# Experts' biases: 128-row products for gate and up, one sum over all tokens for down, and four pairs of split weights beside nine raw slots

## The chip, the cores and the metric

The kernel runs on one core of one Trainium2 chip. The metric is the device time of one execution in microseconds (us). The engines are named as in the profile: PE (TensorE, its matmuls; PEld its weight loads), DVE (VectorE), ACT (ScalarE), POOL (GpSimd) and SP (SyncE, which issues most of the DMAs).

## The reference, cut to what matters

The program computes one block with four mixers and a routed feed-forward part, and then a second block of two layers. The change touches the feed-forward part of the first: 512 tokens of 1024 features, 32 experts, four experts for each token.

```python
logits = (x2d @ router_w + router_b).astype(jnp.float32)
top_val, top_idx = lax.top_k(logits, TOP_K)
gate = jax.nn.softmax(top_val, axis=-1)
...
hg, hl = jnp.split(xblk @ w_gu[e] + b_gu[e], 2, axis=-1)
hg = jnp.minimum(hg, SWIGLU_LIMIT)
hl = jnp.clip(hl, -SWIGLU_LIMIT, SWIGLU_LIMIT)
glu = hg * jax.nn.sigmoid(hg * SWIGLU_ALPHA)
return ((hl + 1.0) * glu) @ w_down[e] + b_down[e]
...
y = (yb * row_gate[:, None]).astype(x2d.dtype)
return jnp.zeros((t + 1, d), x2d.dtype).at[row_tok].add(y)[:t]
```

All of it is float32 and is kept at nearly that precision: a float32 operand is cut into a high and a low part of the type float32r, and a product is the sum of three (high times high, low times high, high times low).

## The kernel before

`block1_ffn` holds the part in question. It first makes the output projection, the layer norm and the router for the four token tiles, then runs over the 32 experts, then adds a gated embedding and a second norm by token tile.

An expert has 96 slots for tokens (`NS`). `slots` finds the tokens of an expert's slots: four one-hot tiles `o1` (L1378), four small bf16 products (L1380), and a few narrow vector operations that give the index `ix`, the destination `dx` and the gate `gc`. It also makes `sel`, a tile of 64 rows whose columns all have a one at rows e and 32 + e (L1375, on POOL, from `eye2`). `rows` gathers the tokens (`xg`, L1397) and transposes them into two parts `xT` (`transposed`, L1227 on PE, L1228 on ACT, L1229 on DVE).

`main` computes the expert. For each half q of the hidden features and for gate and up, it begins a bank `gu` with the product of `sel` and `bias` (L1411: 64 rows, high and low parts of all the experts' biases, one above the other), and adds 8 blocks of 128 features by `mm3` (L1148 to L1150, three products each of 512 columns). Then come, for each half, `hg` (L1421, DVE, from the gate bank), `sg` (L1422, ACT), `hg` times `sg` (L1424, POOL), `hl` (L1423, DVE, from the up bank), `hl` again (L1425, DVE), and the transposition of `hl` into `hT`. The down product `py` begins with two products of `sel` and `bdn` (L1432, 64 rows), and adds 2 times 8 blocks by `mm3`. `y` is `py` times the gate, and an indirect DMA adds it to the rows of `h_d` (L1444). The last expert goes another way: `last` keeps its rows in two parts, and `add_last` (L1501 on) adds them by one-hot products to the token tiles.

The weights come in units of 128 by 2048 float32 (1 MB), 12 for each expert: 8 for gate and up, 4 for down. SP issues the loads (L1201) in the order of use into slots that take turns: 6 in the ring, 1 and `N_SPARE` more, in all 11 (L1636). `unit` splits each: ACT copies it to `wh` (L1210), DVE subtracts to get `wl` (L1211). There are `N_PARTS` pairs of `wh` and `wl`, three. So a raw slot is free when `wl` is done, and a pair is free when PE has done the unit's 12 products.

The order of the instructions on each engine is fixed when the program is built, by a scheduler that has its own estimates of what each takes; at run time an engine runs its list in that order and waits where an operand isn't there. So PE passes from one expert to the next without a stop: between the products of one expert stand the biases, transposes and one-hot products of the next.

Of the kernel before, what the change touches and what calls it, by code (L numbers as in the profile page):

```python
# [8 lines left out]
F32 = mybir.dt.float32  # L9
F32R = mybir.dt.float32r  # L10
# [9 lines left out]
D = 1024  # L20
# [3 lines left out]
# ---------------------------------------------------------------- host layout  # L24
# Feature tiles (128 output columns of w_in each) and token-major groups (256).
# [7 lines left out]
FT = [  # name, columns (-1: zero)  # L33
# [93 lines left out]
def layout(inp):  # L127
    """The inputs laid out for the loads: transposed, cut and padded with zeros."""
# [59 lines left out]
    # experts, in units in the order of use: half, gate or linear, k half; k half, half  # L188
# [10 lines left out]
# ---- second block: 16 meta tokens and 512 tokens, 528 in all  # L199
# [18 lines left out]
def _ret_cols(base, j, f=None):  # L218
    """columns of a tile with heads 2j, 2j+1: halves of 24 at rows 0, 32 and 64, 96"""
# [25 lines left out]
def _ret_tables():  # L245
    """rotary tables with the decay gamma^(t - 264) (q) and gamma^(264 - t) / sqrt(dk) (k) folded in"""
# [19 lines left out]
def layout2(inp, o):  # L266
# [6 lines left out]
    o["w2o"] = ft(I("w_out"))          # [2, 8, 128, 8, 128]  # L273
    o["w21"] = ft(I("w_ffn1"))         # [2, 22, 128, 8, 128]
    o["w23"] = ft(I("w_ffn3"))
    w2 = I("w_ffn2").reshape(2, 22, 128, 8, 128)
    part = lambda a: np.ascontiguousarray(a.transpose(0, 3, 2, 1, 4))   # [2, 8, 128, tiles, 128]
# [46 lines left out]
# ---------------------------------------------------------------- device  # L324
# [30 lines left out]
def softplus_steps(k, pool, z, out):  # L355
    """out = softplus(z) = max(z, 0) + log1p(exp(-|z|))"""
# [17 lines left out]
def block1_mix(k, es_mix):  # L374
    """In-projection and the four mixers. Returns their outputs side by side, feature-major
    [128, 8, 512], in two float32r parts, in a pool of es_mix."""
    nc, tc, A = k.nc, k.tc, k.A
    V, ACT, G, PE = nc.vector, nc.scalar, nc.gpsimd, nc.tensor
    with ExitStack() as es:
# [28 lines left out]
        def wt(shape, name, bufs=1):  # L408
            """working tile; the larger ones share slots by size"""
# [44 lines left out]
        def tproj(name, evac):  # L454
            """one token tile at each step"""
# [24 lines left out]
        def tgate(name):  # L480
            """u * sigmoid(u)"""
# [21 lines left out]
        def conv(name, cw, cb, j, out):  # L503
            """out = silu(causal conv of width 4)"""
# [11 lines left out]
        # ---- row quantities: dt and the cumulated decay (SSD), gates (mLSTM)  # L516
# [38 lines left out]
        def post_norm(y, nh, eps, center, gname, mi, between=None, fast=False):  # L555
            """per-head norm over the features of y [128, NCH, 256] in place; then
            transposed into mix tiles mi, mi+1, with the gain (if gname)."""
# [34 lines left out]
        # ---- SSD  # L592
        def ssd():
# [6 lines left out]
            al = wt([128, NCH, 4], "al")     # exp(A_last), over all partitions  # L600
            dc = wt([128, NCH, 4], "dc")     # exp(A_last - A_s)
            ea = wt([128, NCH, 4], "ea")     # exp(A_t)
# [52 lines left out]
        # ---- GLA  # L655
        def gla():
# [15 lines left out]
            sc = wt([128, NCH], "gl_sc")     # state: end of chunk c to the middle of c+1  # L672
# [55 lines left out]
        # ---- mLSTM  # L728
        def mlstm():
# [11 lines left out]
            # the gate as tanh(u / 2) = 2 sigmoid(u) - 1  # L741
# [48 lines left out]
        # ---- the mixers' outputs and the weights of the output projection, two float32r parts each  # L790
# [8 lines left out]
        def out_piece(n, i):  # L799
            """two blocks of rows of half n of the columns"""  # L800
# [352 lines left out]
def block1_ffn(k, mix, wo, es_mix, b2):  # L1153
# [5 lines left out]
    with es:  # L1159
# [73 lines left out]
        with tile_pool(tc, name="w1", bufs=1) as w1:  # L1233
# [14 lines left out]
            for i in range(2):  # L1248
                nc.sync.dma_start(braw[32 * i:32 * i + 32], A["b_gu"])
# [1256 lines left out]
```

## Time and profile before

| | |
|---|---|
| time, median of 3 runs | 3178.87 us (3176.96 to 3190.85) |
| span of the profiled execution | 3183.1 us |
| PE busy | 3025.6 us, 95% of the span |
| DVE busy | 2144.0 us, 67% |
| ACT busy | 1533.5 us, 48% |
| POOL busy | 819.9 us, 26% |
| first `hg` of the first expert, of the last expert's second half | 488.7 us, 1717.0 us |

The share of busy time is taken over the whole span, whose stages differ. The experts take from about 450 to 1735 us. A matmul's own duration in a row is longer than the distance to the next one's start, since they overlap, so the cost of a product is read from the distance of the starts.

### The profile page before, as it was taken

The page shows a single profiled execution, that of the slowest core. Times are in us where ns is not written, and L with a number is a line of the kernel's source. Part 1 is how long each engine was busy: PE and PEld are TensorE (multiplying, and loading weights), DVE is VectorE, ACT ScalarE, POOL GpSimd, SP SyncE. Part 2 cuts the span into 40 slices and gives each one's busy share as a digit, 9 for nine tenths or more (in the row PEclk, how much of TensorE's full clock was granted, in tenths as well). Part 3 has the DMA queues.
Part 4 walks back from the last instruction along what each step waited for, and adds up shares of the span by engine and source line. Part 5 has one row for each costly group of instructions (what it writes and reads, how often), then busy time and mean ns, then how long its engine had stood idle before and what let it go on. Part 6 is the DMA issues. An engine that isn't in the chain of part 4 may idle for free. (4 is left out here: it accounts for less than half of the span.)

```text
span 3183.1 us, 45711 instructions
## 1 busy us (share of the span) xinstructions
PE 3025.6 (95%) x18347; PEld 2488.6 (78%) x18347; DVE 2144.0 (67%) x3036; ACT 1533.5 (48%) x1840; POOL 819.9 (26%) x538
## 2 busy tenths in 40 slices
PE   6899879999999999999999899999999899999997
PEld 4799666666666666666666788999999899999997
DVE  4745758999999989799988766653333846834324
ACT  4411426677766666676666644342222534432222
POOL 1210233333333333234322320320102501410104
PEclk8989889999999999999999989999999889999998
DMA  3201268999999999799997121122222211222221
GB/s 121 73 21 41 85 255 319 340 348 350 351 353 340 343 343 334 300 351 344 343 343 244 51 91 41 65 82 91 84 93 80 95 45 50 80 97 90 97 85 52
DMA packets 105991, 581.58 MB, mean 183 GB/s; under 512 B 13016, under 2 KB 13544, under 8 KB 55792
## 3 DMA queue, kind: packets, MB, share of 16 engines
q1 hardware_dynamic: 94784, 540.86, 45.9%
q0 software_dynamic: 10896, 37.52, 4.4%
q8 instruction: 145, 2.38, 0.3%
q14 instruction: 70, 0.57, 0.1%
q10 hardware_dynamic: 96, 0.26, 0.0%
HBM read 559.64 MB, written 18.94 MB: 182 GB/s over the span
## 5 line engine op out<-in xcount | busy, mean ns | idle before, releaser
L1211 DVE TENSOR_TENSOR wl<-w,wh 128x2048 fp32r<-128x2048 f32 (+1 forms) x398 | 909.3, 2293 | 85.0 <-ACT wh L1210 84.0
L1210 ACT ACTIVATE wh<-w 128x2048 fp32r<-128x2048 f32 (+1 forms) x410 | 734.1, 1808 | 133.2 <-PE gu L1150 87.1
L1775 PE MATMUL gu<-hh,w 128*128 128x256 f32 (+2 forms) x1552 | 454.6, 293 | 8.3 <-ACT hh L2473 8.3
L1776 PE MATMUL gu<-hl,w 128*128 128x256 f32 (+2 forms) x1552 | 451.3, 291 | 3.5 <-DVE hl L2475 2.7
L1777 PE MATMUL gu<-hh,w 128*128 128x256 f32 (+2 forms) x1552 | 449.1, 290 | 0.8 <-DVE w L1142 0.8
L1149 PE MATMUL gu<-wl,xT 128*96 128x512 f32 x1024 | 414.6, 405 | 8.8 <-DVE wl L1211 7.4
L1148 PE MATMUL gu<-wh,xT 128*96 128x512 f32 x1024 | 406.1, 397 | 0.2 <-ACT wh L1210 0.2
L1150 PE MATMUL gu<-wh,xT 128*96 128x512 f32 x1024 | 403.9, 394 | 0.0
L1142 DVE TENSOR_TENSOR w<-w 128x1024 fp32r<-128x1024 f32 (+1 forms) x190 | 237.6, 1251 | 234.1 <-ACT w L1141 229.8
L1141 ACT ACTIVATE w<-w 128x1024 fp32r<-128x1024 f32 (+1 forms) x194 | 201.2, 1038 | 259.5 <-PE gu L2299 84.6
L1775 PEld LDWEIGHTS gu<-hh,w 128*128 128x128 f32 x1552 | 300.6, 194 | 11.0 <-ACT hh L2473 9.9
L1776 PEld LDWEIGHTS gu<-hl,w 128*128 128x128 f32 x1552 | 300.0, 193 | 6.6 <-DVE hl L2475 4.4
L1777 PEld LDWEIGHTS gu<-hh,w 128*128 128x128 f32 x1552 | 300.9, 194 | 2.0 <-DVE w L1142 1.3
L1424 POOL TENSOR_TENSOR hg<-hg,sg 96x512 f32<-96x512 f32 x64 | 171.5, 2680 | 333.7 <-ACT sg L1422 333.7
L1149 PEld LDWEIGHTS gu<-wl,xT 128*96 128x96 f32 x1024 | 165.3, 161 | 106.6 <-DVE wl L1211 33.2
L2284 POOL TENSOR_TENSOR al<-fs,ah 128x528 fp32r<-128x528 f32 (+1 forms) x44 | 76.7, 1744 | 608.1 <-ACT ah L2283 608.1
L1148 PEld LDWEIGHTS gu<-wh,xT 128*96 128x96 f32 x1024 | 165.9, 162 | 73.4 <-issue 1.9
L1150 PEld LDWEIGHTS gu<-wh,xT 128*96 128x96 f32 x1024 | 165.8, 162 | 62.6
L1149 PE MATMUL py<-wl,hT 128*96 128x512 f32 x512 | 206.5, 403 | 0.2
L1148 PE MATMUL py<-wh,hT 128*96 128x512 f32 x512 | 204.3, 399 | 0.1
L1150 PE MATMUL py<-wh,hT 128*96 128x512 f32 x512 | 200.9, 397 | 0.0
L1444 POOL DMA_INDIRECT h_d<-y,dx x31 | 119.1, 3840 | 226.2 <-ACT y L1443 222.2
(701 smaller groups left out, 6478.0 us busy)
## 6 DMA issues: line engine op xcount, KB each, us to landing
w<-in_wgu SPq DMA_DIRECT2D x255, 1024.0 KB, 7.3
w<-in_wdn SPq DMA_DIRECT2D x127, 1024.0 KB, 6.5
w<-in_w SPq DMA_DIRECT2D x88, 512.0 KB, 3.5
w<-in_w2f SPq DMA_DIRECT2D x43, 512.0 KB, 3.7
w<-in_w22a SPq DMA_DIRECT2D x32, 512.0 KB, 3.8
w<-in_w1f SPq DMA_DIRECT2D x18, 512.0 KB, 3.5
w<-in_w2o SPq DMA_DIRECT2D x16, 512.0 KB, 3.6
w<-in_w22b SPq DMA_DIRECT2D x16, 384.0 KB, 3.4
```

What stands on the lines that cost most here:

```text
L1141: nc.scalar.activation(h, w, AF.Copy)
L1142: (eng or nc.vector).tensor_sub(l, w, h.bitcast(F32))
L1148: PE.matmul(out, a[0], b[0], start=start, stop=False)
L1149: PE.matmul(out, a[0], b[1], start=False, stop=False)
L1150: PE.matmul(out, a[1], b[0], start=False, stop=stop)
L1210: ACT.activation(h[:, j], w[:, j], AF.Copy)
L1211: (early or V).tensor_sub(l[:, j], w[:, j], h[:, j].bitcast(F32))
L1424: G.tensor_mul(hg, hg, sg)
L1444: G.indirect_dma_start(out=h_d, out_offset=bass.IndirectOffsetOnAxis(ap=dx[:, :1], axis=0), in_=y, in_offset=None, compute_op=OP.add)
L1775: PE.matmul(p, w[0][:, kk], x[0][:, kk, c], start=kk == ks[0], stop=False)
L1776: PE.matmul(p, w[0][:, kk], x[1][:, kk, c], start=False, stop=False)
L1777: PE.matmul(p, w[1][:, kk], x[0][:, kk, c], start=False, stop=kk == ks[-1])
```

## The change

- The biases of gate and up lie in `bias` as 128 rows of bf16: three parts one below the other (32 rows each, the rest of the rest), and 32 rows of zeros. `sel` has 128 rows of bf16 with three ones in each column. The product at the head of each `gu` bank thus has 128 rows instead of 64, and bf16 instead of float32r operands. Making the parts takes one copy on ACT, three subtractions and three casts of 32 by 2048 on DVE and a memset on POOL, where there was one copy and one subtraction. One DMA more brings the biases.
- The two products of `sel` and `bdn` are gone from each expert. The down biases are added once: `gates`, after the third expert's hidden features are there, transposes the gates of all tokens (four copies side by side) into `GT`, in parts; `add_last` begins each of its 8 banks with the product of `GT` and `bdn`, which now has 128 rows (high, high, low, low).
- `N_PARTS` goes from 3 to 4, `N_SPARE` from 4 to 2: four pairs of split weights, nine raw slots.
- `strict` has a tile and a DMA of its own. The loop over further blocks of experts, which is not run with these inputs, is changed to match.

Line numbers behind the diff differ from those above by 11 to 22. The comments, which the changed file drops, are left out.

```diff
-        bias = cons.tile([64, 2048], F32R, name="bias")
+        bias = cons.tile([128, 2048], BF, name="bias")
+        Gm = cons.tile([128, NCH, N_EXP], F32, name="Gm")
+        bdn = fcst.tile([128, D], F32R, name="bdn")
+        GT = fcst.tile([128, NCH, 128], F32R, name="GT")
...
-            braw = raw(rows=64)
-            for i in range(2):
+            braw = raw(rows=96)
+            for i in range(3):
                 nc.sync.dma_start(braw[32 * i:32 * i + 32], A["b_gu"])
-            ACT.activation(bias, braw, AF.Copy)
-            V.tensor_sub(bias[32:64], braw[32:64], bias[32:64].bitcast(F32))
+            ACT.activation(bias[0:96], braw, AF.Copy)
+            G.memset(bias[96:128], 0.0)
+            for i in range(1, 3):
+                b_, w_ = bias[32 * i:32 * i + 32], braw[32 * i:32 * i + 32]
+                for _ in range(i):
+                    V.tensor_sub(w_, w_, b_)
+                    V.tensor_copy(b_, w_)
...
-            for i in range(2):
+            for i in range(4):
                 nc.scalar.dma_start(bd[32 * i:32 * i + 32], A["b_dn"])
             ACT.activation(bdn, bd, AF.Copy)
-            V.tensor_sub(bdn[32:64], bd[32:64], bdn[32:64].bitcast(F32))
+            V.tensor_sub(bdn[64:128], bd[64:128], bdn[64:128].bitcast(F32))
+
+        def gates():
+            p = bank("tr", (128, 4, 128))
+            for t in range(NCH):
+                g4 = wb.tile([128, 128], F32, name="g4")
+                G.tensor_copy(g4.rearrange("p (a b) -> p a b", a=4), Gm[:, t][:, None, :].to_broadcast([128, 4, N_EXP]))
+                PE.transpose(p[:, t], g4, ident)
+            ACT.activation(GT, p, AF.Copy)
+            for i in (32, 96):
+                V.tensor_sub(GT[i:i + 32], p[i:i + 32], GT[i:i + 32].bitcast(F32))
...
-                sel = sm.tile([64, NS], F32R, name="sel", bufs=3)
-                eng.tensor_copy(sel, idc.to_broadcast([64, NS]))
+                sel = sm.tile([128, NS], BF, name="sel", bufs=3)
+                eng.tensor_copy(sel, idc.to_broadcast([128, NS]))
...
                 py = [bank("py", (NS, 512)) for _ in range(2)]
-                for n in range(2):
-                    PE.matmul(py[n], sel, bdn[:, 512 * n:512 * n + 512], start=True, stop=False)
...
-                            mm3(PE, py[n], (hT[0][:, a], hT[1][:, a]), (h[:, j], l[:, j]), False, a == 7)
+                            mm3(PE, py[n], (hT[0][:, a], hT[1][:, a]), (h[:, j], l[:, j]), a == 0, a == 7)
...
                     p = bank("py")
+                    PE.matmul(p, GT[:, t], bdn[:, 512 * n:512 * n + 512], start=True, stop=False)
                     for i in range(2):
-                        PE.matmul(p, oh[:, t], yp[:, D * i + 512 * n:D * i + 512 * n + 512], start=i == 0, stop=i == 1)
+                        PE.matmul(p, oh[:, t], yp[:, D * i + 512 * n:D * i + 512 * n + 512], start=False, stop=i == 1)
...
-                     {1: further, 20: embedding}.get(e), last if e == k.n_exp - 1 else None)
+                     {1: further, 2: gates, 20: embedding}.get(e), last if e == k.n_exp - 1 else None)
...
-N_RAW, N_SPARE, N_PARTS = 6, 4, 3
+N_RAW, N_SPARE, N_PARTS = 6, 2, 4
```

**On PE, in the middle of the experts.** Before, where the transposes of the next expert's tokens begin (`tr<-fcst,xg`), one of that expert's four gate and up biases (L1411) follows the transposes:

```order
L1148 MATMUL py<-wh,hT_7700 96x512
L1227 MATMUL tr<-fcst,xg 128x96 x4
L1411 MATMUL gu<-bias,sel 96x512
L1149 MATMUL py<-wl,hT_7700 96x512
L1150 MATMUL py<-wh,hT_7701 96x512
```

After, at the same place:

```order
L1148 MATMUL py<-wh,hT_7397 96x512
L1230 MATMUL tr<-fcst,xg 128x96 x4
L1433 LDWEIGHTS sel
L1433 MATMUL gu<-bias,sel 96x512
L1149 MATMUL py<-wl,hT_7397 96x512
```

The bias keeps its place among the products; as a bf16 product it has a weight load of its own in the list.

**On PE, a little later, where the down products of one expert end and the gate products of the next begin.** Before, one of the two down biases (L1432) stands behind the first gate product:

```order
L1149 MATMUL py<-wl,hT_7700 96x512
L1150 MATMUL py<-wh,hT_7701 96x512
L1148 MATMUL gu<-wh,xT_7658 96x512
L1432 MATMUL py<-bdn,sel 96x512
L1149 MATMUL gu<-wl,xT_7658 96x512
```

After:

```order
L1149 MATMUL py<-wl,hT_7397 96x512
L1150 MATMUL py<-wh,hT_7398 96x512
L1148 MATMUL gu<-wh,xT_7355 96x512
L1149 MATMUL gu<-wl,xT_7355 96x512
L1150 MATMUL gu<-wh,xT_7356 96x512
```

Nothing takes the place of the down bias.

**On DVE, in the start, around the second token tile's norm.** Before, one subtraction (L1251) for the biases stands between the two halves of that norm (L1103, L1104):

```order
L1103 SCALAR_TENSOR_TENSOR x<-x,rn_mv,g_3007 128x1024
L1251 TENSOR_TENSOR bias<-w,bias 32x2048
L1104 SCALAR_TENSOR_TENSOR x<-x,rn_rs,b_3008 128x1024
L1268 SCALAR_TENSOR_TENSOR x<-x,gu 128x512
L1096 BN_STATS rn_st<-x 128x6
L1288 TENSOR_TENSOR lg<-py,rb 128x32
```

After, six operations (L1261 and L1262) stand behind the norm, among the router's steps for that tile and the next tile's norm:

```order
L1104 SCALAR_TENSOR_TENSOR x<-x,rn_rs,b_3011 128x1024
L1279 SCALAR_TENSOR_TENSOR x<-x,gu 128x512
L1261 TENSOR_TENSOR w<-w,bias 32x2048 x2
L1262 CAST bias<-w 32x2048 x2
L1299 TENSOR_TENSOR lg<-py,rb 128x32
L1261 TENSOR_TENSOR w<-w,bias 32x2048
L1307 MAX m_3249<-lg 128x8
L1279 SCALAR_TENSOR_TENSOR x<-x,gu 128x512
L1262 CAST bias<-w 32x2048
```

The subtraction that stood ahead of the norm's second half is behind it, and five more operations stand ahead of the router's steps.

## Rows read from the trace of the kernel before

**Rows 1.** Windows, one expert each (first, second kind): busy us by engine, PE clock, DMA.
```profile
986.40:1025.63 39.23, 38.90 (x171) 25.04 (x170) 35.41 (x33) 26.27 (x20) 14.35 (x7) 1.00 0.96 342
720.25:758.21 37.96, 37.95 (x172) 25.31 (x171) 34.44 (x34) 26.83 (x21) 12.53 (x6) 1.00 0.96 353
```

**Rows 2.** One line's instructions each, L1411, L1432 and L1421: count, duration, first and last start.
```profile
L1411 PE MATMUL gu<-bias,sel x128: 383/466/473, 449.7 to 1688.0; 64*96 64x512 f32 x128
...
L1432 PE MATMUL py<-bdn,sel x64: 383/466/736, 474.6 to 1700.7; 64*96 64x512 f32 x64
...
L1421 DVE TENSOR_SCALAR hg<-gu x64: 673/680/689, 488.7 to 1717.0; 96x512 f32<-96x512 f32 x64
```

**Rows 3.** Timeline of PE, a gate or up bias alone: start, duration, instruction.
```profile
949.99 0.40 PE L1148 MATMUL gu<-wh,xT 128*96 128x512 f32 x1
950.31 0.47 PE L1411 MATMUL gu<-bias,sel 64*96 64x512 f32 x1
950.71 0.47 PE L1149 MATMUL gu<-wl,xT 128*96 128x512 f32 x1
951.02 0.39 PE L1150 MATMUL gu<-wh,xT 128*96 128x512 f32 x1
951.25 0.39 PE L1148 MATMUL gu<-wh,xT 128*96 128x512 f32 x1
```

**Rows 4.** Timeline of PE, two down biases side by side.
```profile
811.82 0.39 PE L1150 MATMUL gu<-wh,xT 128*96 128x512 f32 x1
812.14 0.70 PE L1432 MATMUL py<-bdn,sel 64*96 64x512 f32 x2
812.77 0.47 PE L1148 MATMUL py<-wh,hT 128*96 128x512 f32 x1
813.08 0.39 PE L1149 MATMUL py<-wl,hT 128*96 128x512 f32 x1
```

**Rows 5.** Timeline of PE, transposes and small bf16 products between the large ones.
```profile
826.13 0.49 PE L1227 MATMUL tr<-fcst,xg 96*128 96x96 f32 x4
826.46 0.30 PE L1380 MATMUL tr<-aux,o 128*96 128x6 bf16 x4
826.62 0.45 PE L1148 MATMUL gu<-wh,xT 128*96 128x512 f32 x1
```

**Rows 6.** The page's groups: the weight load of one of the large products.
```profile
L1149 PEld LDWEIGHTS gu<-wl,xT 128*96 128x96 f32 x1024 | 165.3, 161 | 106.6 <-DVE wl L1211 33.2
```

**Rows 7.** Timeline of PE, where a low part comes late.
```profile
992.32 0.40 PE L1148 MATMUL gu<-wh,xT 128*96 128x512 f32 x1
992.86 0.47 PE L1149 MATMUL gu<-wl,xT 128*96 128x512 f32 x1
```

**Rows 8.** Timeline of DVE beside it; in brackets the idle time before and its releaser.
```profile
986.40 0.69 DVE L1421 TENSOR_SCALAR hg<-gu 96x512 f32<-96x512 f32 x1 [1.05 <-PE gu L1150]
987.00 2.28 DVE L1211 TENSOR_TENSOR wl<-w,wh 128x2048 fp32r<-128x2048 f32 x1
989.65 3.15 DVE L1211 TENSOR_TENSOR wl<-w,wh 128x2048 fp32r<-128x2048 f32 x1 [0.37 <-ACT wh L1210]
```

**Rows 9.** Waits from 600 to 1600 us: who waited for whom, us in total, times, longest.
```profile
DVE wl L1211 <- ACT wh L1210: 70.9, 80, 10.6
ACT wh L1210 <- PE gu L1150: 66.0, 84, 1.6
```

**Rows 10.** SP's queue over the same stretch.
```profile
SPq L1201 <- DVE wl L1211: 820.8, 290, 7.0
```

**Rows 11.** Timeline of DVE in the start.
```profile
424.55 2.28 DVE L1251 TENSOR_TENSOR bias<-w,bias 32x2048 fp32r<-32x2048 f32 x1
...
443.98 0.19 DVE L1288 TENSOR_TENSOR lg<-py,rb 128x32 f32<-128x32 f32 x1 [3.94 <-PE py L1286]
```

**Rows 12.** Windows of 4 us inside the second kind of expert, columns as in rows 1.
```profile
736.00:740.00 4.00, 4.00 (x18) 2.50 (x17) 4.00 (x3) 1.98 (x2) 1.51 (x2) 1.00 1.02 422
...
752.00:756.00 4.00, 4.00 (x19) 2.80 (x18) 4.00 (x9) 3.23 (x2) 2.23 (x1) 1.00 0.58 158
```

More of the change, by code (lines that the diff above doesn't have):

```diff
@@ L1164, in block1_ffn @@
         fcst = pool("fcst", 1)
-        cst = fcst.tile([128, 256], F32, name="fcst")
+        ident = fcst.tile([128, 128], F32, name="fcst")
         pool_x = lambda n: es_x.enter_context(tile_pool(tc, name=n, bufs=1))
@@ L1171, in block1_ffn @@
         cst2 = cons.tile([128, 129], F32, name="fcst2")
-        ident, strict, iota, pidx = cst[:, 0:128], cst[:, 128:256], cst2[:, 0:128], cst2[:, 128:129]
-        bias = cons.tile([64, 2048], F32R, name="bias")
+        iota, pidx = cst2[:, 0:128], cst2[:, 128:129]
+        bias = cons.tile([128, 2048], BF, name="bias")
+        Gm = cons.tile([128, NCH, N_EXP], F32, name="Gm")
+        bdn = fcst.tile([128, D], F32R, name="bdn")
+        GT = fcst.tile([128, NCH, 128], F32R, name="GT")
         Rm = cons.tile([128, NCH, N_EXP], F32, name="Rm")
@@ L1207, in unit @@
             n = w.shape[1]
-            h, l = ((p or parts).tile([128, 4, 512], F32R, name=i, tag=i, bufs=1 if p else N_PARTS)[:, :n] for i in ("wh", "wl"))
+            h, l = (parts.tile([128, 4, 512], F32R, name=i, tag=i, bufs=N_PARTS)[:, :n] for i in ("wh", "wl"))
             for j in [slice(i, i + 1) for i in range(n)] if early else [slice(0, n)]:
@@ L1242, in block1_ffn @@
             nc.sync.dma_start(b1, bcast(A["rows2"], D, D))
-            nc.sync.dma_start(cst, A["cst"][:, 0:256])
+            strict = w1.tile([128, 128], F32, name="strict")
+            nc.sync.dma_start(ident, A["cst"][:, 0:128])
+            nc.sync.dma_start(strict, A["cst"][:, 128:256])
             nc.sync.dma_start(cst2, A["cst"][:, CF["iota"][0]:CF["iota"][0] + 129])
@@ L1255, in block1_ffn @@
             G.memset(ob_, 1.0)
-            eye2 = sm.tile([64, 32], F32, name="eye2")
-            V.tensor_add(eye2, ident[:64, 0:32], ident[:64, 32:64])
+            eye3 = sm.tile([128, 32], F32, name="eye3")
+            V.tensor_add(eye3, ident[:, 0:32], ident[:, 32:64])
+            V.tensor_add(eye3, eye3, ident[:, 64:96])
             M = w1.tile([128, NCH, N_EXP], F32, name="M")
             Mb = w1.tile([128, NCH, N_EXP], BF, name="Mb")
-            Gm = w1.tile([128, NCH, N_EXP], F32, name="Gm")
             for t in range(NCH):
@@ L1336, in block1_ffn @@
             wb = es_b.enter_context(tile_pool(tc, name="wb", bufs=1, side="right"))
-            bd = w1.tile([128, 8, 128], F32, name="x1T", bufs=2).rearrange("p a b -> p (a b)")[:64]
-            bdn = parts.tile([64, D], F32R, name="bdn")
-            for i in range(2):
+            bd = w1.tile([128, 8, 128], F32, name="x1T", bufs=2).rearrange("p a b -> p (a b)")
+            for i in range(4):
                 nc.scalar.dma_start(bd[32 * i:32 * i + 32], A["b_dn"])
             ACT.activation(bdn, bd, AF.Copy)
-            V.tensor_sub(bdn[32:64], bd[32:64], bdn[32:64].bitcast(F32))
+            V.tensor_sub(bdn[64:128], bd[64:128], bdn[64:128].bitcast(F32))
[8 more added lines that the diff above has]
+                V.tensor_sub(GT[i:i + 32], p[i:i + 32], GT[i:i + 32].bitcast(F32))
         def further():
@@ L1446, in main @@
                 return res
-            first = lambda e: slots(lambda t: Rm[:, t, e:e + 1], lambda t: aux[:, t, e], eye2[:, e:e + 1], G if e else V)
+            first = lambda e: slots(lambda t: Rm[:, t, e:e + 1], lambda t: aux[:, t, e], eye3[:, e:e + 1], G if e else V)
             def embedding():
@@ L1537, in block1_ffn @@
                     axe = ex.tile([128, NCH, 1, 6], BF, name="axe", bufs=1)
-                    ide = ex.tile([64, 1], F32, name="ide", bufs=1)
+                    ide = ex.tile([128, 1], F32, name="ide", bufs=1)
                     jc = ex.tile([128, 1], F32, name="jc", bufs=1)
@@ L1541, in block1_ffn @@
                     V.tensor_copy(axe, aux[:, :, bass.ds(e, 1)])
-                    V.tensor_copy(ide, eye2[:, bass.ds(e, 1)])
+                    V.tensor_copy(ide, eye3[:, bass.ds(e, 1)])
                     V.tensor_copy(jc, tblj[:, bass.ds(b, 1)])
```

## The prediction

> **What bounds the kernel now.** I read the windows first, one for each of two kinds of expert [rows 1]. Each runs from the first `hg` of one expert to that of the next, so its length is an expert's share of the time: 39.23 us for the one kind, 37.96 us for the other. In both PE is busy nearly throughout (38.90 and 37.95 us) at clock 1.00. DVE is not far behind: 35.41 and 34.44 us. ACT (26 us) and POOL (13 to 14 us) are not near. So PE sets the pace in this stage and DVE would be next, and the change takes work from PE there. Of the 31 distances from one expert to the next (64 `hg`, first and last in [rows 2]) 13 are of the first kind, 12 of the second, and 6 are others: the first two, and those around the embedding's projection.
>
> A busy PE is not PE at its peak, so I then read the starts of its products. Two plain products start 0.23 us apart (951.02 and 951.25 [rows 3]). A product of 64 rows between them takes more than its own place: the distance before it is 0.32, behind it 0.40, and the next one 0.31 us. From 949.99 to 951.02 that is 1.03 us for three products of which two are plain (0.46), so a bias that stands alone costs 0.57 us [rows 3]. Two side by side cost less: 1.26 us from 811.82 to 813.08, less two plain ones, is 0.80, or 0.40 each [rows 4].
>
> PE also waits a little. At 992.32 the distance to the next product is 0.54 instead of 0.23 us [rows 7]: that product needs `wl`, which DVE has in work just then, for 3.15 us instead of 2.28, and which it began late because `wh` was late [rows 8]. `wh` in turn waits for PE to give a pair free [rows 9]. This is a ring of three pairs with no room in it. An expert of the first kind has two such places, some 0.6 us together.
>
> **Gate and up biases.** 128 products of 64 rows [rows 2] become 128 of 128 rows. What a bf16 product of 128 rows and 512 columns costs among float32r ones, no row shows. From below it is a plain product, 0.23. From above it is what the 64-row one costs, 0.57, if the other type and not the fewer rows is what lengthens the distances. The nearest rows are the four small bf16 products of 128 rows that follow four transposes: 0.16 us for all four [rows 5]. They speak for the lower end, and I take 0.23. That saves 0.34 for a bias that stood alone and 0.17 for one of a pair: 4 x 0.34 = 1.4 us in an expert of the first kind, where all stand alone, and some 0.8 in one of the second.
>
> **Down biases.** 64 products go: 2 x 0.57 = 1.1 us in an expert of the first kind, 0.8 in one of the second. What takes their place lies outside the loop: eight products of 128 rows in `add_last`, 1.8 to 3.2 us by 0.23 and 0.40, some of it beside waits; I take +1.7. `gates` runs once: four transposes (0.33 by [rows 5], wider here) and two narrow DVE operations, at most 0.69 each as `hg` with the same 512 columns [rows 8]. That is 0 to 2; I take +0.5.
>
> **Fourth pair, two raw slots fewer.** A fourth pair lets ACT and DVE run one unit further ahead, which is 12 products or 2.8 us of PE. The late places (0.6 us) should go, and much of DVE's own waiting for `wh` (70.9 us over some 26 experts [rows 9]). The price is in the loads. SP's queue waits for a free slot nearly always, 820.8 us in 290 waits over 1000 us [rows 10], so loads run as far ahead as the slots permit. At 3 us for a unit, nine slots come round after 27 us where eleven took 33, and a load of 1 MB takes 2.5 us at the 422 GB/s that are reached where slots are free; where they are not, the rate falls to 158 [rows 12]. So the mean of 342 to 353 GB/s [rows 1] is set by the slots coming free. An expert in 36.6 us wants 353 x 37.96 / 36.6 = 366 GB/s. I take zero for this, and the rival below is its other end.
>
> **The new pace.** PE's own floor is 148 products of 0.231, 34.2 us, four groups of transposes of 0.33, 1.3 us, and the small bf16 products with what follows them, 0.4: 36.0 us. The savings above give much the same: 39.23 - 1.4 - 1.1 - 0.6 = 36.1, and 37.96 - 1.6 = 36.4. DVE keeps its work in the loop, 35.4 us [rows 1], and sits idle for 3.8 now. From below the pace is 36.0; from above 37.3, when half of that idle time stays. I take 36.6, which is 35.4 with about the one wait of 1.05 us for the gate products [rows 8], since `hg` keeps its place in DVE's list: nearer PE's end, because the ring then has room.
>
> **The start.** On DVE one subtraction of 2.28 us [rows 11] becomes three and three casts: at most 5 x 2.28 = 11.4 us more, at least 4.6, if casts cost next to nothing. They lie among the router's steps of the second and the norms of the next tiles, where DVE waited 3.94 us for PE [rows 11]; so the last tile's norm, from which the gather and the first expert follow, comes at most 7.5 us later. The second tile's norm is rid of the subtraction in its middle, which can bring what follows 2.28 us forward. From -2 to +7.5; I take +2, nearer the lower end, because a cast has one operand to read where the subtraction has two.
>
> **The sum.** First kind: 39.23 - 36.6 = 2.63, times 13 is 34.2. Second: 37.96 - 36.6 = 1.36, times 12 is 16.3. Six others at about 1.5: 9.0. Together 59.5 off; less 1.7, 0.5 and 2.0 it is 55.3. The profiled execution's own span of 3183.1 becomes 3127.8. The median of the runs shown, 3178.9, lies 4.2 lower, so the forecast is 3178.9 - 55.3 = 3123.6, say 3123.
>
> **A rule on weight loads.** A large product has a weight load of 161 ns [rows 6], and these products start 0.23 us apart all the same [rows 3]: the load lies wholly beside the product before. The Trainium skill's page "TensorE: Matmul & The Clock Gate", section "The mechanism" of its part on packing small matmuls, says that a weight load overlaps products in flight only where it goes to other rows of the array. By that no load for all 128 rows would be hidden, the new bias's either. Rows 3 and 6 don't agree with it for float32r; for a bf16 load among float32r products no row shows it, so it stands as a rival.
>
> **Rivals.**
> - *DVE sets the pace*, 37.3 us. For it: DVE's 35.4 us of work, and `wl` slowed to 3.15 us beside POOL's product [rows 8]. Against it: much of its idle time is the wait for `wh`, which the fourth pair shortens. 13 x 1.9 + 12 x 0.7 + 6 x 0.8 = 37.9 off, less 4.2: 3145.
> - *PE at its floor*, 36.0 us: 13 x 3.2 + 12 x 2.0 + 6 x 2.0 = 77.6 off, less 4.2: 3105. For it: the sums by parts above.
> - *The bias's weight load isn't hidden*, as it is bf16 among float32r: 0.16 us for each of 128 is 20 us back: 3143.
> - *It doesn't do what it says*: a bf16 product of 128 rows costs 0.57 as the 64-row one did. Then the down biases are gained, 13 x 1.1 + 12 x 0.8 + 6 x 1.0 = 29.9, and the late places, 13 x 0.6 = 7.8, less 4.2: 3145. [Rows 5] speak against it.
> - *The loads starve the split.* If the mean rate stays at 353 GB/s, an expert takes its 37.96 us of loads, and only the first kind gains: 13 x 1.27 = 16.5, less 4.2: 3167. Against it stands the rate of 422 GB/s [rows 12].
> - *Slower: the transposes of `hl` come late.* In each half of an expert PE's list has them a fixed number of products behind the up bank's end, and `hg`, `sg`, POOL's product and `hl` must be through by then. Without the dear biases PE gets there sooner, and with a fourth pair a further `wl` can be ready and stand in front of `hl`. If PE waited for one `wl` of 2.28 us [rows 8] at each of the 64 places, that is 146 us: 3178.9 + 146 - 55.3 = 3270. It decides from 55.3 / 64 = 0.9 us at each. Against it: DVE's list is fixed, and it would take a third `wl` between `hg` and `hl` there.
>
> **How the numbers follow.** Chances: the forecast 0.57; DVE sets the pace 0.17; PE at its floor 0.08; the load not hidden or the bias as dear as before 0.07; starved loads 0.06; slower 0.05. The forecast's own bounds are 3109 to 3138: the pace at 0.3 us to either side is 9 us, the start 4 to 6 more. For 8 in 10 the range takes in the rivals at 3143 to 3145 with some of the start's bound, and PE's floor, and leaves out the starved loads and the slower case: 3105 to 3152. Faster by over 0.5%, about what a measurement of this kernel can tell from no change, is under 3163; slower is over 3195. Starved loads count as the same: faster 0.88, same 0.07, slower 0.05.
>
> **What would show it.** In the changed kernel's trace the distances around the new bias should be 0.23 us; the rivals say 0.39 or 0.57 for it. The window of one expert should be near 36.6 us, with PE busy throughout and DVE at 35 us in it. If PE waits at `wl`, DVE sets the pace; if it waits at the transposes of `hl`, it is the slower case; if `wh` waits for a DMA, the loads starve. ACT's `wh` should hardly wait for PE any more. The start is right if the first `hg` comes between 2 us before and 7.5 us after 488.7 us [rows 2]. The whole is wrong if the experts' stage keeps its length.

## The result, and the profile after

The changed kernel takes 3158.73 us (median of 4 runs, 3154.27 to 3164.83) beside 3182.96 for the kernel before (4 runs, 3176.96 to 3190.85): ratio 0.9923, 95% interval 0.9898 to 0.9947. So it is faster, but by 24 us and not by the 55 of the forecast, and its time lies above the range.

The two profiled executions differ by more, 3183.1 and 3152.6 us. Part of that isn't the change's. In the mixers, whose instructions the change doesn't touch, PE ran at a clock of 0.66 in the one profile and of 1.00 in the other. First the kernel before, then after, the stretch from 200 to 240 us (length, busy us of PE, PEld, DVE, ACT, POOL with counts, PE clock, DMA share, GB/s):

```profile
200.00:240.00 40.00, 40.00 (x223) 37.62 (x222) 9.45 (x22) 5.24 (x11) 7.63 (x12) 0.66 0.08 27
```
```profile
200.00:240.00 40.00, 39.48 (x311) 37.16 (x311) 15.11 (x33) 7.89 (x16) 7.61 (x12) 1.00 0.17 53
```

At the lower clock 223 products fit into the 40 us, at the higher one 311. The output projection, which follows, began at 394.19 us before and at 382.52 after. Both kernels' runs lie at two levels some 10 us apart, so times below are compared over several runs, and places in the trace by the distance between two events of one stage.

From that first product on, the profiles give this:

| stretch | before | after | difference | forecast |
|---|---|---|---|---|
| first product of the output projection to the first expert's `hg` | 94.5 | 90.5 | -4.0 | +2 |
| first expert's `hg` to the last expert's | 1215.3 | 1197.6 | -17.7 | -59.5 |
| last expert's `hg` to the end | 1479.2 | 1481.9 | +2.8 | +2.2 |

Together -18.9; with the -11.7 ahead of it that is, but for rounding, the difference of the spans. **The miss lies in the middle row.** One steady expert of after, from its first `hg` to the next one's (columns as above; [rows 1] has its counterpart):

```profile
1043.57:1081.99 38.42, 37.49 (x169) 24.77 (x168) 35.13 (x33) 26.02 (x20) 13.21 (x6) 1.00 0.97 342
```

38.4 us instead of 39.2, where 36.6 was forecast. PE's busy time fell by 1.4 us, from 38.90 to 37.49, but idle time came back: 0.93 us where there was 0.33. The new bias is not to blame. The products around one, where nothing is late (PE's timeline: start, duration):

```profile
1046.15 0.39 PE L1148 MATMUL gu<-wh,xT 128*96 128x512 f32 x1
1046.38 0.38 PE L1433 MATMUL gu<-bias,sel 128*96 128x512 bf16 x1
1046.51 0.47 PE L1149 MATMUL gu<-wl,xT 128*96 128x512 f32 x1
1046.82 0.40 PE L1150 MATMUL gu<-wh,xT 128*96 128x512 f32 x1
```

From 1046.15 to 1046.82 is 0.67 us for three products of which two are plain (0.46): the bias costs 0.21, where [rows 3] gave 0.57 for the old one. The forecast was 0.23.

Three microseconds on a low part is late, as in [rows 7]: 0.67 us to the next product instead of 0.23.

```profile
1049.15 0.40 PE L1148 MATMUL gu<-wh,xT 128*96 128x512 f32 x1
1049.82 0.47 PE L1149 MATMUL gu<-wl,xT 128*96 128x512 f32 x1 [0.28 <-DVE wl L1214]
```

Over the stretch from 600 to 1600 us of after (who waited for whom, us in total, times, longest; [rows 9] and [rows 10]):

```profile
DVE wl L1214 <- ACT wh L1213: 52.9, 82, 9.5
ACT wh L1213 <- PE gu L1150: 21.0, 27, 1.1
PE gu L1149 <- DVE wl L1214: 17.9, 54, 1.3
```
```profile
SPq L1204 <- DVE wl L1214: 844.9, 301, 12.3
```

`wh` waits for PE to free a pair for a third of the time that it did: the fourth pair does that. But DVE waits for `wh` nearly as often as before (82 times, 80 before). The pair was not what it waited for. What it was shows on the timelines of one expert's first half, DVE first, then ACT (in brackets the idle time before and its releaser):

```profile
1043.57 0.69 DVE L1443 TENSOR_SCALAR hg<-gu 96x512 f32<-96x512 f32 x1 [0.68 <-PE gu L1150]
1044.18 2.28 DVE L1214 TENSOR_TENSOR wl<-w,wh 128x2048 fp32r<-128x2048 f32 x1
1046.82 2.94 DVE L1214 TENSOR_TENSOR wl<-w,wh 128x2048 fp32r<-128x2048 f32 x1 [0.37 <-ACT wh L1213]
1049.69 0.68 DVE L1445 TENSOR_SCALAR hl<-gu 96x512 f32<-96x512 f32 x1
1050.48 0.69 DVE L1447 SCALAR_TENSOR_TENSOR hl<-hl,hg 96x512 f32<-96x512 f32 x1
1051.08 2.28 DVE L1214 TENSOR_TENSOR wl<-w,wh 128x2048 fp32r<-128x2048 f32 x1
1053.29 0.55 DVE L1232 TENSOR_TENSOR hT<-tr,hT 128x384 fp32r<-128x384 f32 x1
1054.38 2.29 DVE L1214 TENSOR_TENSOR wl<-w,wh 128x2048 fp32r<-128x2048 f32 x1 [0.55 <-ACT wh L1213]
```
```profile
1044.35 0.63 ACT L1444 ACTIVATE sg<-hg 96x512 f32<-96x512 f32 x1 [2.85 <-DVE hg L1443]
1044.89 3.70 ACT L1213 ACTIVATE wh<-w 128x2048 fp32r<-128x2048 f32 x2
1052.06 0.49 ACT L1231 ACTIVATE hT<-tr 128x384 fp32r<-128x384 f32 x1 [3.47 <-PE tr L1230]
1052.45 3.71 ACT L1213 ACTIVATE wh<-w 128x2048 fp32r<-128x2048 f32 x2
```

ACT stands idle for 2.85 us, then does `sg`, then the `wh` for which DVE waits 0.37 us. It stands idle for 3.47 us, then does the copy of `hT`, then the `wh` for which DVE waits 0.55 us. It is idle with pairs free and with the weights there: where the trace of a steady expert has a load's landing, it lies 13 to 18 us before the load's split. The high parts stand *behind* `sg` and `hT` in ACT's list, `sg` waits for `hg`, and `hT` for PE's transposes, which in turn wait for DVE's `hl`. So DVE waits for ACT, and ACT waits for DVE and PE. In the kernel before the same two waits are 0.37 [rows 8] and 0.55 us, behind the same two instructions of ACT (its DVE, then its ACT):

```profile
997.43 2.29 DVE L1211 TENSOR_TENSOR wl<-w,wh 128x2048 fp32r<-128x2048 f32 x1 [0.55 <-ACT wh L1210]
```
```profile
987.18 0.64 ACT L1422 ACTIVATE sg<-hg 96x512 f32<-96x512 f32 x1 [2.22 <-DVE hg L1421]
987.72 3.71 ACT L1210 ACTIVATE wh<-w 128x2048 fp32r<-128x2048 f32 x2
995.10 0.49 ACT L1228 ACTIVATE hT<-tr 128x384 fp32r<-128x384 f32 x1 [3.67 <-PE tr L1227]
```

**The theory (A):** a ring through the order of ACT's list, not through the pairs, the slots or PE, sets the pace; so the change's saving on PE turns largely into PE waiting for low parts. **The rivals:** DVE's own work sets the pace (B); the two raw slots given up hold the loads back (C); the new bias costs more than the rows around it show (D). The expectations below were written with letters of their own: their B is that PE's own work still sets the pace, which is nearest to D here, and their B2 is B here.

### The profile page after: what moved, and what is told of

Same layout as the page of the kernel before. It is cut to its first block, busy times and chain, and to the rows that moved or that the text cites. A ratio compares the mean times of both kernels' runs of the same rounds, so it can differ in the third digit from the quotient of the medians.

```text
span 3152.6 us, 45612 instructions
## 1 busy us (share of the span) xinstructions
PE 2975.8 (94%) x18295; PEld 2471.6 (78%) x18295; DVE 2152.6 (68%) x3044; ACT 1521.8 (48%) x1838; POOL 831.8 (26%) x543
## 5 line engine op out<-in xcount | busy, mean ns | idle before, releaser
L1213 ACT ACTIVATE wh<-w 128x2048 fp32r<-128x2048 f32 (+1 forms) x410 | 726.1, 1805 | 64.8 <-PE gu L1150 42.4
L1464 POOL DMA_INDIRECT h_d<-y,dx x31 | 128.8, 4154 | 191.1 <-ACT y L1463 185.9
```

The costliest lines, as they stand in the source:

```text
L1213: ACT.activation(h[:, j], w[:, j], AF.Copy)
L1464: G.indirect_dma_start(out=h_d, out_offset=bass.IndirectOffsetOnAxis(ap=dx[:, :1], axis=0), in_=y, in_offset=None, compute_op=OP.add)
```

## The experiments

Times are medians. "Stage" is the profiled stretch from the first expert's `hg` to the last expert's, "pace" a steady expert's share of it, both in us; the ratio is to the kernel before, in the same comparison.

| kernel | us | ratio (95%) | stage | pace |
|---|---|---|---|---|
| before | 3183 to 3186 | 1 | 1215.3 | 39.2 |
| after | 3158.7 | 0.9923 (0.9898 to 0.9947) | 1197.6 | 38.4 |
| e1_copies_ahead | 3125.5 | 0.9836 (0.9792 to 0.9880) | 1168.5 | 37.0 |
| e2_no_gate_up_bias | 3152.5 | 0.9912 (0.9883 to 0.9941) | 1189.1 | 38.0 |
| e3_biases_alone | 3165.2 | 0.9943 (0.9916 to 0.9969) | 1193.3 | 38.4 |
| e4_pairs_alone | 3191.5 | 1.0020 (0.9997 to 1.0043) | 1222.4 | 39.2 |
| e5_before_pairs_ahead | 3175.8 | 0.9980 (0.9963 to 0.9997) | 1210.3 | 38.5 |
| e6_down_as_rows | 3167.8 | 0.9951 (0.9933 to 0.9969) | 1196.9 | 38.6 |
| e7_three_pairs_ahead | 3138.4 | 0.9871 (0.9833 to 0.9910) | 1174.1 | 37.0 |
| e8_cheap_low_parts | 3122.3 (one run) | | 1168.4 | 37.2 |
| e9_two_ahead | 3139.2 | 0.9864 (0.9844 to 0.9884) | 1172.9 | 37.1 |
| e10_two_ahead_of_sigmoid | 3123.0 | 0.9815 (0.9794 to 0.9837) | 1158.4 | 36.4 |

### The list alone: e1_copies_ahead

The edit changes the order of ACT's list and no work: one high part more stands ahead of `sg`, and one ahead of the copy of `hT`, in all experts but the one beside the embedding (`behind(i)` puts an instruction behind the high part of the expert's unit i). The lists of the other engines are built around it and move too. In a steady expert DVE's second `wl` behind `hl` now stands ahead of `hT`, where it stood behind it, and the second four of PE's transposes of `xg` come later among the down products. So the run tries an order of the lists, set through ACT's.

```diff
+                 def un(i):
+                     while len(made) <= i:
+                         n_ = len(made)
+                         made[n_] = (*(wg(n_) if n_ < 8 else wd(n_ - 8)), copies[0])
+                     return made[i]
+                 def behind(i):
+                     return tc.issue_after(un(i)[2].ins) if ahead_ok else nullcontext()
...
-                    ACT.activation(sg, hg, AF.Sigmoid, scale=1.702)
+                    with behind(4 * q + 4):
+                        ACT.activation(sg, hg, AF.Sigmoid, scale=1.702)
...
-                    last = transposed(hl, hT[0][:, 4 * q:4 * q + 4], hT[1][:, 4 * q:4 * q + 4])
+                    with behind(4 * q + 6):
+                        last = transposed(hl, hT[0][:, 4 * q:4 * q + 4], hT[1][:, 4 * q:4 * q + 4])
```

> The changed kernel, but in each half of an expert (from the third on, except the one with the embedding's projection) ACT makes one more high part before it takes the sigmoid, and one more before it copies the transposed hidden features. Theory A (the experts' pace is a ring between DVE and ACT: in each half DVE waits 0.37 and 0.55 us for a high part that stands behind the sigmoid and behind the transposes in ACT's list): these waits go, a steady expert falls from 38.4 to about 36.6 us and the whole by 25 to 37 us. Rival B (PE still sets the pace, and the biases cost more than one plain product): no change within 5 us. Rival C (nine raw slots: loads come too late): no change, or DVE and ACT now wait for loads.

Measured: 3125.52 us, pace 37.0; the pace expected was 36.6, and the gain lies inside its 25 to 37 us. The same half on DVE (timeline as above), and the window of a steady expert:

```profile
1073.50 0.69 DVE L1456 TENSOR_SCALAR hg<-gu 96x512 f32<-96x512 f32 x1
1074.11 4.48 DVE L1216 TENSOR_TENSOR wl<-w,wh 128x2048 fp32r<-128x2048 f32 x2
1079.32 0.69 DVE L1459 TENSOR_SCALAR hl<-gu 96x512 f32<-96x512 f32 x1 [0.73 <-PE gu L1150]
```
```profile
1036.46:1073.50 37.04, 36.48 (x169) 24.78 (x168) 33.73 (x32) 26.13 (x21) 17.40 (x6) 1.00 0.98 362
```

The wait of 0.37 us is gone, both subtractions run in 4.48 us, and now DVE waits for PE ahead of `hl`, as it should where PE sets the pace. No work was taken away, and 33 us went. This speaks for A and against C and D: the loads keep 362 GB/s with the nine slots, and the same bias stands in a pace 1.4 us shorter. DVE's own busy time fell as well, from 35.13 to 33.73 us; the section on the hardware says why. That is the whole 1.4 us of the pace: DVE's idle time is 3.3 us in both, but where it waited for ACT it now waits for PE. No run takes away the slower `wl` and leaves the waits, so what each of the two is worth by itself stays open.

### The biases without cost: e2_no_gate_up_bias

```diff
-                        PE.matmul(p, sel, bias[:, 1024 * gl + 512 * q:1024 * gl + 512 * q + 512], start=True, stop=False)
```

> The changed kernel without the 128 products that add the gate and up biases (these biases are left out of the result). Theory A: PE has room, so a steady expert stays at 38.2 to 38.4 us and the whole gains under 8 us. Rival B: 4 x 0.23 us or more for each expert, 37.5 us for a steady one, 29 us in the whole. Rival C: no change.

This kernel leaves the gate and up biases out. Measured: 3152.49 us, pace 38.0, a little under the 38.2 to 38.4 expected. Four products of 0.21 to 0.23 are gone, some 0.9 us, and the pace is 0.4 shorter. Its window has PE idle for 1.3 us of 38.04:

```profile
1019.19:1057.23 38.04, 36.74 (x165) 24.23 (x164) 35.13 (x32) 26.14 (x20) 12.69 (x5) 1.00 0.95 351
```

A bias that costs nothing gives 6 us, which is all that D could have explained of the missing 31. Where the ring is closed, PE's savings count only in part.

### Each part alone: e3_biases_alone, e4_pairs_alone

The first is the changed kernel with the old pools, the second the kernel before with the new ones.

```diff
-N_RAW, N_SPARE, N_PARTS = 6, 2, 4
+N_RAW, N_SPARE, N_PARTS = 6, 4, 3
```

> The change of the biases alone: three pairs of split weights and eleven raw slots as before. Theory A: the fourth pair is hardly used in the steady part, since ACT's list is the same there; a steady expert takes 38.4 us here too, and the whole is within 10 us of the changed kernel. Rival C (the slots taken away cost what the biases gain): faster than the changed kernel by over 10 us. If the fourth pair is what brings the gain: slower than the changed kernel by over 10 us.

> The kernel before with four pairs and nine raw slots, its biases as they were (the loop over further blocks, which is not run, takes its split weights from the same pool). Theory A: a steady expert stays near 39.2 us and the whole within 10 us of before. If the pair is what brings the gain: faster than before by over 15 us. Rival C: slower than before.

Measured: 3165.2 and 3191.5 us, paces 38.4 and 39.2. The biases alone give the changed kernel's pace to the tenth, and the pairs alone give the pace of before. So the whole gain is the biases', and the fourth pair bought nothing here. Nor did the slots cost anything that the times can tell: the interval of e4 reaches from 0.9997 to 1.0043. The profiled stage, one profile each, is 7.1 us longer in e4 than before, and 4.3 us longer in after than in e3. A steady expert of e4 shows why on DVE: with four pairs the wait for `wh` stands where it stood in [rows 8], at the same 0.37 us.

```profile
1031.67 2.28 DVE L1211 TENSOR_TENSOR wl<-w,wh 128x2048 fp32r<-128x2048 f32 x1
1034.32 3.15 DVE L1211 TENSOR_TENSOR wl<-w,wh 128x2048 fp32r<-128x2048 f32 x1 [0.37 <-ACT wh L1210]
```

### The list with the old biases: e5_before_pairs_ahead

The kernel before with `N_RAW, N_SPARE, N_PARTS = 6, 2, 4` and the edit of e1.

> The kernel before with its dear biases, four pairs and nine raw slots, and ACT's list moved as in the first experiment (one more high part ahead of the sigmoid and of the transposes in each half). Theory A: once the ring between DVE and ACT is open, PE's work sets the pace, and the dear biases then cost their full price: a steady expert takes 37.0 plus about 1.5 to 2.1 us, 38.5 to 39.1, hardly less than the 39.2 of before, and the whole is 35 to 60 us above the first experiment. Rival B2 (DVE sets the pace in the opened ring too): a steady expert at 37.0 to 37.4 us, and the whole within 12 us of the first experiment.

Measured: 3175.81 us, pace 38.5. The window of a steady expert:

```profile
1057.15:1095.64 38.49, 38.45 (x171) 25.26 (x170) 33.72 (x32) 26.12 (x20) 16.28 (x6) 1.00 0.97 345
```

PE is busy for 38.45 of 38.49 us, with DVE at 33.72: here, with the ring opened and the old biases, PE is what bounds, as far as busy time tells. Beside e1's 37.04 the pace differs by 1.45 us. PE's busy time differs by 1.97 (38.45 and 36.48), and by 2.30 from e10's below (36.15), where the biases' terms promised 2.5. Busy time is a rough measure (38.90 and 38.45 in before and here, for the same products), but most of the saving that was forecast on PE is there. Of it 1.45 us reach the pace with e1's lists. The four cases together:

| pace, us | ACT's list as it was | high parts ahead |
|---|---|---|
| old biases | 39.2 | 38.5 (e5) |
| new biases | 38.4 | 37.0 (e1) |

The new biases are worth 0.8 in the left column and 1.5 in the right one, the new list 0.7 in the upper row and 1.4 in the lower.

### The down biases in the loop: e6_down_as_rows

The two products of `sel` and `bdn` are put back into each expert, as bf16 ones of 128 rows; `gates` and what follows it go.

```diff
                 py = [bank("py", (NS, 512)) for _ in range(2)]
+                for n in range(2):
+                    PE.matmul(py[n], sel, bdn[:, 512 * n:512 * n + 512], start=True, stop=False)
```

> The changed kernel, but the down biases stay in each expert, as two bf16 products of 128 rows (three parts and zeros), instead of one sum at the end. Theory A: 0.46 us more on PE for each expert, of which less than half is on the ring: a steady expert at 38.4 to 38.6 us, the whole within 6 us of the changed kernel. Rival B: 38.9 us, the whole 13 to 15 us slower than the changed kernel.

Measured: 3167.78 us, pace 38.6, which is 0.2 more than after's 38.4. Two products of 0.21 to 0.23 would be 0.45; again half of it shows. The whole was expected within 6 us of after; the medians differ by 9, with intervals that overlap, and the profiled stage is 0.7 us shorter. So of the down biases' part most was to be had by the cheaper form of the product, and little by moving the sum out of the loop.

### Three pairs with the list: e7_three_pairs_ahead

> The new biases and ACT's list moved as in the first experiment, with three pairs and eleven raw slots. Theory A in its full form (the list and the fourth pair only pay together): the earlier high part has no pair free when its turn comes, so the sigmoid behind it waits, and a steady expert takes 38.4 us or more. If the list alone is what counts: 37.0 us as in the first experiment.

This is e1 with three pairs and eleven slots. Measured: 3138.36 us, pace 37.0. I had thought by then that the list and the fourth pair pay only together. That fell: with three pairs the pace is the same 37.0, although `wh` waits for PE again:

```profile
ACT wh L1215 <- PE gu L1150: 115.7, 128, 1.7
DVE wl L1216 <- ACT wh L1215: 41.4, 20, 11.7
```

115.7 us of ACT's waiting cost the steady pace nothing, and DVE waits 20 times instead of 82. The stage is 5.6 us longer than e1's, and the intervals of the two ratios overlap. Whether the lists of e10 below would do with three pairs was not run.

### Less work on DVE: e8_cheap_low_parts

Two of an expert's twelve subtractions, those of units 4 and 8, become copies with one operand. The low parts that they leave are not the true ones.

```diff
-                (early or V).tensor_sub(l[:, j], w[:, j], h[:, j].bitcast(F32))
+                if cheap and not early:
+                    V.tensor_copy(l[:, j], w[:, j])
+                else:
+                    (early or V).tensor_sub(l[:, j], w[:, j], h[:, j].bitcast(F32))
```

> The changed kernel, in which DVE makes the low parts of units 4 and 8 of each expert by a copy instead of a subtraction (these two low parts are wrong, PE's and ACT's work is the same). These are the low parts that PE waits for in each half. Theory A: the copy takes some 1.2 us instead of 2.3 to 2.9, the ring is that much shorter, and a steady expert falls from 38.4 to 36.2 to 37.0 us. Rival B: no change beyond 0.3 us.

Measured: 3122.34 us in one run, pace 37.2. A copy takes 1.22 us and not 2.28, and the window has DVE at 31.70 of 37.19 us:

```profile
1032.74:1069.93 37.19, 36.84 (x169) 24.69 (x168) 31.70 (x33) 26.15 (x20) 15.16 (x6) 1.00 0.97 360
```

The pace falls by 1.2 us, a little less than expected. It would be B's claim that less work on DVE did it. But the copy reads `w` alone, so it waits for no `wh` either, and the 0.37 us are gone with the work:

```profile
1033.35 2.28 DVE L1217 TENSOR_TENSOR wl<-w,wh 128x2048 fp32r<-128x2048 f32 x1
1035.55 1.22 DVE L1215 CAST wl<-w 128x2048 fp32r<-128x2048 f32 x1
```

So this run can't part B from A. What speaks against B is e5: DVE has 35.13 us to do in after, where the pace is 38.4, and 33.72 in e5 and 33.73 in e1, where the paces are 38.5 and 37.0. The last two have the same lists in a steady expert but for the biases. DVE's work is one side of the ring, not the bound by itself.

### Further ahead: e9_two_ahead, e10_two_ahead_of_sigmoid

e9 puts a second high part ahead of both `sg` and the copy of `hT`; e10 ahead of `sg` alone. The edit of e9 against e1 (e10 has its first half):

```diff
-                    with behind(4 * q + 4):
+                    with behind(4 * q + 5):
                         ACT.activation(sg, hg, AF.Sigmoid, scale=1.702)
...
-                    with behind(4 * q + 6):
+                    with behind(4 * q + 7):
                         last = transposed(hl, hT[0][:, 4 * q:4 * q + 4], hT[1][:, 4 * q:4 * q + 4])
```

> As the first experiment, but ACT makes two more high parts ahead of the sigmoid and two ahead of the transposes, which only four pairs permit; DVE's list then has one low part between the two steps of the hidden features that were back to back. If the fourth pair can still open the ring further: a steady expert at 36.0 to 36.6 us (PE's floor), 12 to 30 us off the first experiment. If DVE's place for the hidden features decides (the prediction's slower mechanism): PE waits at their transposes, a steady expert at 37.5 us or more, slower than the first experiment.

> Two more high parts ahead of the sigmoid, one ahead of the transposes. Same question: 36.0 to 36.6 us for a steady expert if the pairs are what is left to use, 37.0 us or more if the chain of the hidden features is, with PE's waits then at their transposes.

Measured: 3139.2 and 3123.0 us, paces 37.1 and 36.4. A steady expert of e10:

```profile
1040.86:1077.35 36.49, 36.15 (x169) 24.83 (x168) 33.61 (x33) 26.12 (x21) 13.72 (x6) 1.00 0.99 368
```

PE is busy for all but 0.34 us, near the floor of 36.0 that the prediction gave. e10 is the fastest kernel over the stage, 39 us below after, and its interval does not touch after's. e9 lies between the two answers that it was to decide. In the steady part its PE doesn't wait at the transposes, but once in a steady expert at a down product, 0.8 us for a `wl` (who waited for whom from 1040 to 1240 us):

```profile
PE py L1149 <- DVE wl L1216: 4.1, 5, 0.8
```

e10 has no such wait in that stretch, and its pace is 0.7 us shorter. That the later copy of `hT` makes this `wl` late is argued, not shown.

## Why the prediction was right or wrong

- **PE sets the pace now: half right.** PE was busy in 38.90 of 39.23 us [rows 1], and DVE was called next. In fact DVE, ACT and PE stood in a ring of much the same length in the first kind of expert; e5 shows what PE needs there with the old biases, 38.5.
- **Gate and up biases, 0.23 each: right.** Measured 0.21 to 0.23 where nothing is late, where the old one cost 0.57. The rivals that had it at 0.39 and 0.57 fall, and e2 shows that even a bias for nothing would not have mended the forecast.
- **The weight load of the new bias: hidden.** The load is in the trace, and the products around it keep their distances (one line's loads: shortest, median, longest in ns):

```profile
L1433 PEld LDWEIGHTS <-sel x128: 120/121/180, 433.7 to 1655.5; 128*96 128x96 bf16 x128
```

  The Trainium skill's page "TensorE: Matmul & The Clock Gate", section "The mechanism", names beside other rows of the array a second case in which a load is drawn ahead, a background buffer for weights; the prediction had left that case out. By the rule as I told it the bias would cost 0.12 us more. The 0.21 shows it doesn't, for bf16 among float32r products too.
- **Down biases: right in sign.** e6 puts cheap ones back and loses 0.2 an expert.
- **Fourth pair: wrong, and this is the step that failed.** I read the late places and DVE's waits for `wh` as the shortage of pairs, because `wh` waited for PE [rows 9]. Those were two different sets of waits. The two lines are from before, seven experts of the second kind (606.86 to 872.14 us), where no low part is late, and seven of the first (986.40 to 1260.95 us), where two are:

```profile
ACT wh L1210 <- PE gu L1150: 33.7, 44, 0.9
```
```profile
ACT wh L1210 <- PE gu L1150: 6.0, 7, 0.9
```

  The pairs' share did fall, 66.0 to 21.0 us, and bought nothing (e4); the 0.37 us that mattered [rows 8] was `wh` standing behind `sg` on ACT. The rows to see it were in the trace of before: who releases ACT just ahead of the late `wh`. I read what `wh` waits for over the whole stage, and not what ACT did before this `wh`.
- **The new pace, 36.6: wrong by 1.8 in the first kind,** as a consequence. It took nearly all that PE saved as saved, "because the ring then has room"; the ring stayed closed, with PE idle for 0.93 us. While the ring is closed a third to a half counts: 0.8 of the 2.0 to 2.3 us that the biases take from PE, 0.4 of 0.9 in e2, 0.2 of 0.45 in e6. With the list opened the pace is 36.4 (e10), and the time 3123, the number that was forecast for the change without it; that doesn't make the forecast right. (The floor's terms, 34.2, 1.3 and 0.4, add up to 35.9 and not 36.0, which changes nothing.)
- **The sum by kinds of expert.** It kept each expert in its kind, and that didn't hold. Before had 13 of the first kind; after has 16 at 38.4 to 38.7, among them some in places where before had 37.5 to 38.0. The first twelve distances, most of them of the second kind before, came down by only 3.8 us together (458.7 to 455.0), the other nineteen by 14.0. The second kind itself gained nearly what was forecast. e3, with the old pools, keeps it longer, and there it runs at 36.8 us for six experts in a row, where [rows 1] has 37.96. Its lists, as built and with no edit, have a high part ahead of the first `sg`, and ACT doesn't stand idle ahead of `hT` (e3, one expert's window, and ACT in it):

```profile
727.48:764.28 36.80, 36.38 (x170) 24.91 (x169) 34.84 (x33) 26.59 (x20) 11.80 (x6) 1.00 0.98 365
```
```profile
728.32 1.92 ACT L1213 ACTIVATE wh<-w 128x2048 fp32r<-128x2048 f32 x1 [0.86 <-PE gu L1150]
730.14 0.62 ACT L1444 ACTIVATE sg<-hg 96x512 f32<-96x512 f32 x1
...
738.49 0.47 ACT L1231 ACTIVATE hT<-tr 128x384 fp32r<-128x384 f32 x1
```

  So in one and the same execution the same biases give 36.8 us with one order of the lists and 38.4 with the other.
- **The start: wrong in sign, and outside its bounds of -2 to +7.5.** Only the operations came out inside theirs. They take 10.6 us where there were 2.28 [rows 11], so 8.3 more, between the 4.6 and the 11.4 of the forecast:

```profile
416.49 4.59 DVE L1261 TENSOR_TENSOR w<-w,bias 32x2048 f32<-32x2048 f32 x2
421.12 2.47 DVE L1262 CAST bias<-w 32x2048 bf16<-32x2048 f32 x2
423.84 2.28 DVE L1261 TENSOR_TENSOR w<-w,bias 32x2048 f32<-32x2048 f32 x1
426.97 1.22 DVE L1262 CAST bias<-w 32x2048 bf16<-32x2048 f32 x1
```

  But the distance from the output projection's first product to the first `hg` shrank by 4.0 us. It varies from 89.8 to 96.8 us among the profiles of all these kernels, so a few us of it are not the change's to explain.
- **The rivals.** The time lies between "the loads starve" (3167) and "DVE sets the pace" (3145). The mechanism of the first is excluded by e1 and e3, and that of the second is a part of what was found, so the time falling near it is no support for it: PE waits at `wl`, as it said one would see, but because of what stands ahead of `wh`. "Slower", by late transposes of `hl`, did not come about.

## What to carry to other kernels

Where two engines hand work to each other, ask of each late operand what its engine did just before, and what released that: an operand may be late because it stands in an in-order list behind an instruction that waits for the very engine that wants it. Then more buffers don't help (e4), and less work on the busiest engine counts only in part. So try the order of the lists first (e1: no work removed, 33 us); behind it the same saving was worth nearly twice as much (1.5 us an expert instead of 0.8). And ask of a wait in which kind of stretch it stands, before the sum over a stage is read as one cause.

## What the runs showed of the hardware

**A two-operand subtraction on DVE and POOL's product get in each other's way.** POOL's product of `hg` and `sg` in after, alone, and where it began beside a `wl` behind which DVE has the gap of 0.37 us; then in e1, where two `wl` run without a gap (POOL's timelines):

```profile
598.26 1.29 POOL L1446 TENSOR_TENSOR hg<-hg,sg 96x512 f32<-96x512 f32 x1
...
1045.07 2.55 POOL L1446 TENSOR_TENSOR hg<-hg,sg 96x512 f32<-96x512 f32 x1 [0.83 <-ACT sg L1444]
```
```profile
1075.00 4.75 POOL L1460 TENSOR_TENSOR hg<-hg,sg 96x512 f32<-96x512 f32 x1 [0.19 <-ACT sg L1458]
```

1.29 us becomes 2.55 and 4.75. In after, the `wl` beside which it begins ends at 1046.46 (1044.18 and 2.28), in e1 the two end at 1078.59 (1074.11 and 4.48); the product ends 1.16 us behind either, so it seems to have got nowhere while they ran. In e1 they lost nothing. In after, the next `wl` began inside those 1.16 us and took 2.94 instead of 2.28. So in these rows whichever has begun is served, and the gap that ACT's list leaves costs DVE 0.37 us and then 0.66 more. Twice an expert 0.66 is 1.3 of the 1.4 us by which DVE's busy time falls in e1. The Trainium skill's page "VectorE: DVE Perf Modes", section "Two Vector instructions with no wait between them", says that the second of two SBUF operands is read through an interface that Vector shares with GpSimd; these rows agree, and price it.

**A product of 64 rows among ones of 128 costs more than one of 128 rows:** 0.57 us [rows 3] against 0.21. The runs change rows and type together, so which of them does it stays open. The Trainium skill's page "TensorEngine Tiling (Array Packing)", section "Key Properties", says that a change of tiling mode drains the engine, which fits the distances on both sides of the old bias.

**The granted clock differed between two profiles over the same instructions:** 1.00 is the 2.4 GHz level, and 0.66 a mean over 40 us in part of which the 1.2 GHz level was granted. PE was busy for all of the 20 us before, at 1.00, in both profiles. All that follows the mixers shifted by 11.7 us, half of what the change is worth.
